# Attention in which the exponentials are transposed by the plain identity and the outputs are divided by the softmax sums once per eight heads

## The chip, the cores and the metric

The kernel runs on one core of a Trainium2 chip. The metric is the device time of one execution in microseconds, as the median of several runs.

## The reference, cut to what matters

Two layers of a diffusion backbone over 512 latent tokens ("lat", four tiles of 128) and 256 context tokens ("ctx", two tiles), model width 1024, everything in float32. Each layer has attention in two head groups, an output projection, and an expert retrieval (PEER). For the change only the two attentions count:

```python
# group A, 8 heads: keys are 256 context + 512 latent tokens
s = jnp.einsum('bqhd,bkhd->bhqk', qblk, k_all).astype(jnp.float32) * MLA_QK ** -0.5
p = jax.nn.softmax(s, axis=-1)
o = jnp.einsum('bhqk,bkhd->bqhd', p, v_all)
# group B, 8 heads: context keys + a window of +-128 tokens + one sink logit per head
p = softmax(concatenate([s_ctx, s_loc, s_sink]))      # s scaled by SWA_DIM ** -0.5, the sink not
o = p[..., :C] @ vc + p[..., C:C + nk] @ vblk
```

So each output row of a head is (exponentials times values) divided by the sum of the exponentials, where in group B the sum also has the exponential of the head's sink. Context tokens attend to context alone.

## The kernel before

The work is cut into token tiles of 128. For each tile there are generators: `KV` and `Q` (normalise, project, rotate), `A` (attention, function `attend`), `O` (output projection, line 561), `R` (routing: 16 products with `wq` at line 630 and top-16 searches on VectorE) and `G`/`GH` (choice of experts; one-hot matrices at lines 826 to 840). The main loop strings them together; `par` interleaves two or three of them by weights. There are ten calls of `attend`: two context tiles and four latent tiles in layer 0, four latent tiles in layer 1.

The experts of some tiles are fetched row by row: `experts` issues one indirect transfer of 512 KB per row on GpSimd's queue (line 740) into one of five buffers, and VectorE multiplies it (line 744, a dot product, or line 754, an addition). The experts of the other tiles go through a dense stage (lines 854 to 914), whose order is written out by hand. Nearly half of the gathered rows are issued ahead of the dense stage and fill the time of the stages before it. Outside the dense stage the order of each engine's instructions is set by a planner that simulates the engines; each engine then runs its list strictly in that order.

`attend` goes over four pairs of heads of group A, then four pairs of group B. For each head: the scores go to a `big` accumulator (two of them; lines 526, 541, 544, 547); `soft` takes the row maximum on VectorE (line 476), turns it into a negative bias by one small VectorE instruction (line 482) or, with a sink, two (lines 479 and 480), runs the exponential on ScalarE with the sum as a by-product (line 485), with a sink adds its exponential (lines 488, 489), takes the reciprocal of the sum (line 490) and makes on ScalarE a 128x128 diagonal matrix `dsu` of it (line 492, three buffers). `pair_pv` then turns each 128x128 block of exponentials (line 504): the product of the block with that diagonal matrix is the block transposed and divided by the sums at once. ScalarE copies two blocks of both heads to `peT` (line 508), line 511 multiplies the values by them, and line 513 copies a pair's 128x128 output into `oT`, which `O` reads in eight slices `k`, accumulated in order. The transposes elsewhere (`heads_T`, line 358, and line 464) use the transpose instruction with `ident`. Line 504 is:

```python
nc.tensor.matmul(pt[:, (2 * b + x) * P:(2 * b + x + 1) * P],
                 pe[x][0][:, (b0 + b) * P:(b0 + b + 1) * P], pe[x][1], start=True, stop=True)
```

`pt` is one of two `m1` accumulators, which the routing and the projections use too.

## Time and profile before

| what | value |
|---|---|
| median of 3 runs | 4539.35 us (4536.53 to 4549.56) |
| the profiled execution's own time | 4543.53 us |
| its span, first to last instruction | 4541.7 us |
| mean granted TensorE clock | 0.899 of 2.4 GHz |
| busy: TensorE, VectorE, ScalarE, GpSimd | 82%, 74%, 38%, 37% |
| instructions | 59277, of them 20350 matmuls |

The stretches of attention lie at about 163 to 289 us, 540 to 1284 us and 2757 to 3476 us of the span; the two dense stages lie at about 1400 to 2530 us and 3600 to 4541 us. A share of busy time is a mean over stages with different limits. "The chain" below is the chain of work that ended last, followed back from the last instruction: at each step to what released it, or to the instruction before it on its engine.

### The profile page before, as it was taken

How to read it: one execution, taken by the hardware profiler on the slowest of the kernel's cores; microseconds unless marked ns; L12 is line 12 of the kernel's file. 1: busy time of each engine (PE TensorE's matmuls, PEld its weight loads, DVE VectorE, ACT ScalarE, POOL GpSimd, SP SyncE). 2: the span in 40 equal slices, each digit the busy share in tenths (PEclk: the TensorE clock that was granted, in tenths of full speed). 3: DMA queues.
4: the chain of work that ended last, by engine and by line, in shares of the span. 5: the costliest groups of instructions: out<-in, count | busy, mean ns of one | idle time of the engine just before them, and what ended most of it. 6: DMA issues, size and time to landing. Idle time of an engine off the chain costs nothing.

```text
span 4541.7 us, 59277 instructions
## 1 busy us (share of the span) xinstructions
PE 3707.9 (82%) x20350; PEld 2990.2 (66%) x20350; DVE 3376.4 (74%) x7838; ACT 1731.3 (38%) x3402; POOL 1659.9 (37%) x1402
## 2 busy tenths in 40 slices
PE   6886689478987999999999578677686798888886
PEld 2454358356777888888988445555475787777775
DVE  1247778989678788877888723777997777787887
ACT  1332232156675333333333234233264743333332
POOL 2115565544002444444444500265542014444443
PEclk9987779688987999999999789787887899999998
DMA  8578899889566998999999842798997579999997
GB/s 313 173 248 305 304 336 325 293 313 318 189 211 224 324 322 312 329 326 328 333 313 317 320 150 85 260 343 323 319 337 240 195 265 329 328 331 322 324 321 261
DMA packets 467487, 1306.56 MB, mean 288 GB/s; under 512 B 41568, under 2 KB 147808, under 8 KB 467184
## 3 DMA queue, kind: packets, MB, share of 16 engines
q0 software_dynamic: 199744, 726.26, 45.5%
q1 hardware_dynamic: 267440, 576.50, 36.3%
q8 instruction: 160, 2.62, 0.2%
q14 instruction: 143, 1.17, 0.1%
HBM read 1240.70 MB, written 61.90 MB: 287 GB/s over the span
## 4 chain that ended last, share of the span: by engine, by line
issue 28%; PE 26%; DVE 18%; DMA 11%; POOL 9%; ACT 6%; SPq 0%; POOLq 0%; DVEq 0%; ACTq 0%
POOL gv L740 9%; DVE vacc L754 5%; PE m L630 4%; DMA gv<-v,idx 3%; DVE gv L744 3%; PE m L504 3%; PE m L368 2%; PE A L908 2%; PE o L881 2%; DMA gv<-u,idx 2%; PE m L511 1%; DVE v L855 1%; ACT u L854 1%; DMA w<-w_in 1%; PE big L526 1%
## 5 line engine op out<-in xcount | busy, mean ns | idle before, releaser
L740 POOL DMA_INDIRECT gv<-u,idx x640 | 800.3, 1250 | 1136.5 <-DVE a L744 610.2
L740 POOL DMA_INDIRECT gv<-v,idx x640 | 797.0, 1245 | 931.5 <-DVE vacc L754 593.9
L881 PE MATMUL o<-v,W 128*128 128x512 f32 x3840 | 967.3, 405 | 163.2 <-ACT W L854 161.0
L908 PE MATMUL A<-b,u 128*128 128x384 f32 (+1 forms) x6144 | 954.9, 311 | 21.7 <-ACT w L911 18.7
L908 PEld LDWEIGHTS A<-b,u 128*128 128x128 f32 x6144 | 931.7, 191 | 47.6 <-ACT w L911 25.2
L881 PEld LDWEIGHTS o<-v,W 128*128 128x128 f32 x3840 | 729.1, 194 | 338.7 <-ACT W L854 185.4
L754 DVE SCALAR_TENSOR_TENSOR vacc<-gv,a,vacc 128x1024 f32<-128x1024 f32 x635 | 812.6, 1280 | 51.7 <-DMA gv<-v,idx 39.8
L744 DVE CUSTOM_DVE_ANT_0 gv<-gv,btok 128x1024 f32<-128x1024 f32 x640 | 764.8, 1220 | 77.8 <-DMA gv<-u,idx 75.0
L854 ACT ACTIVATE W<-w 128x384 fp32r<-128x384 f32 (+1 forms) x256 | 120.7, 471 | 1117.3 <-DVE w L914 1117.3
L855 DVE TENSOR_TENSOR u<-raw,u 128x1024 fp32r<-128x1024 f32 x256 | 313.7, 1226 | 161.6 <-ACT u L854 158.9
L368 PE MATMUL m<-w,aT 128*128 128x256 f32 (+3 forms) x704 | 271.1, 536 | 105.7 <-DMA w<-w_in 55.2
L855 DVE TENSOR_TENSOR v<-raw,v 128x1024 fp32r<-128x1024 f32 x256 | 312.2, 1219 | 7.0 <-ACT v L854 7.0
L630 PE MATMUL m<-bT,wq 128*128 128x128 f32 x2560 | 313.1, 278 | 2.2 <-ACT bT L274 1.4
L630 PEld LDWEIGHTS m<-bT,wq 128*128 128x128 f32 x2560 | 300.7, 194 | 7.3 <-issue 4.2
L368 PEld LDWEIGHTS m<-w,aT 128*128 128x128 f32 x704 | 149.9, 223 | 215.7 <-DMA w<-w_in 78.9
L854 ACT ACTIVATE u<-raw 128x1024 fp32r<-128x1024 f32 x256 | 267.6, 1045 | 46.8 <-DMA raw<-uT 46.6
L854 ACT ACTIVATE v<-raw 128x1024 fp32r<-128x1024 f32 x256 | 267.6, 1045 | 9.8 <-PE o L881 8.3
L855 DVE TENSOR_TENSOR W<-w,W 128x384 fp32r<-128x384 f32 (+1 forms) x256 | 126.0, 492 | 151.0 <-ACT W L854 148.5
L504 PE MATMUL m<-dsu,pexp 128*128 128x128 f32 x1472 | 220.9, 294 | 8.0 <-ACT peT L508 5.4
L504 PEld LDWEIGHTS m<-dsu,pexp 128*128 128x128 f32 x1472 | 191.8, 201 | 38.1 <-issue 23.4
L526 PE MATMUL big<-kT,qT 96*128 96x256 f32 (+1 forms) x288 | 140.7, 629 | 69.7 <-ACT pexp L485 52.3
L914 DVE TENSOR_TENSOR w<-w,G 128x192 f32<-128x192 f32 (+1 forms) x512 | 143.6, 320 | 69.9 <-DMA G<-Gd 45.7
(211 smaller groups left out, 4343.4 us busy)
## 6 DMA issues: line engine op xcount, KB each, us to landing
raw<-uT SPq DMA_DIRECT2D x256, 512.0 KB
raw<-v SPq DMA_DIRECT2D x256, 512.0 KB
wq<-wq SPq DMA_DIRECT2D x144, 512.0 KB
gv<-ada_w POOLq DMA_DIRECT2D x80, 512.0 KB
Gd<-ar SPq DMA_DIRECT2D x80, 512.0 KB
w<-w_out SPq DMA_DIRECT2D x72, 512.0 KB
G<-Gd SPq DMA_DIRECT2D x16, 1536.0 KB
G<-Gd SPq DMA_DIRECT2D x16, 1024.0 KB
```

The lines of the kernel that those rows point to most:

```text
L368: nc.tensor.matmul(ps[:, :cn], aT[:, k, :], w[k][:, :cn], start=(k == 0), stop=(k == KC - 1))
L504: nc.tensor.matmul(pt[:, (2 * b + x) * P:(2 * b + x + 1) * P], pe[x][0][:, (b0 + b) * P:(b0 + b + 1) * P], pe[x][1], start=True, stop=True)
L526: nc.tensor.matmul(ps[:, k0:k0 + n], qT[:, h, :], kv["kT"][:, h, k0:k0 + n], start=True, stop=True)
L630: nc.tensor.matmul(ps[:, c], w[:, k, :], bT[:, k, :], start=(k == 0), stop=(k == KC - 1))
L740: return t, nc.gpsimd.indirect_dma_start(out=t, out_offset=None, in_=src, in_offset=bass.IndirectOffsetOnAxis(ap=idx[:, k:k + 1], axis=0))
L744: ins = nc.vector.tensor_tensor_reduce(out=t, in0=t, in1=bt, scale=1.0, scalar=0.0, op0=OP.mult, op1=OP.add, accum_out=a[:, k:k + 1])
L754: return nc.vector.scalar_tensor_tensor(acc, t, w[:, k:k + 1], acc, op0=OP.mult, op1=OP.add)
L854: nc.scalar.activation(hi, x, AF.Copy)
L855: nc.vector.tensor_tensor(lo, x, hi.bitcast(F32), OP.subtract)
L881: nc.tensor.matmul(acc[t][x], W[:, a_, c], v[:, b_, x * 512:(x + 1) * 512], start=(e == 0 and (a_, b_) == PARTS[0]), stop=(e == NK - 1 and ...
L908: nc.tensor.matmul(A, u[:, a_, k * P:(k + 1) * P], b[:, b_, k], start=(k == 0 and (a_, b_) == PARTS[0]), stop=(k == KC - 1 and (a_, b_) == ...
L914: nc.vector.tensor_tensor(wv[:, x], wv[:, x], gc[x][:, :, e % GC, :], OP.mult)
```

## The change

The blocks of exponentials are turned by the transpose instruction with the plain identity, so they stay undivided. The diagonal matrix and the reciprocal per head are gone. The sums of eight heads are collected in one 128x8 tile, and a new function `over_sums`, called twice in each `attend`, takes one reciprocal of the tile, spreads it over the rows of the outputs by eight small products with the identity (values as 64 equal columns, into one `m1` accumulator), and multiplies four 128x128 slices of `oT` by it in place.

The scales of the scores (1/sqrt(96) and 1/sqrt(64)) move into the gains by which the queries are already multiplied as they are copied. With them gone from `soft`, the negated maximum comes straight out of the reduction; in group B one more instruction takes its minimum with the negated sink.

```diff
--- before.py
+++ after.py
@@ -286,15 +286,20 @@
         g = cst.tile([P, n], F32, tag="gains", name="gains")
         src = I["gains"]
         nc.sync.dma_start(g, bass.AP(tensor=src.tensor, offset=src.offset + l * n, ap=[[0, P], [1, n]]))
-        k["sink"] = g[:, 2 * QK + 2 * SD:]
+        k["nsink"] = g[:, 2 * QK + 2 * SD:]
+        nc.vector.tensor_scalar(k["nsink"], k["nsink"], -1.0, None, op0=OP.mult)
         k["g_mq"], k["g_mk"] = g[:, NOPE:QK], g[:, QK + NOPE:2 * QK]
         k["g_sq"], k["g_sk"] = g[:, 2 * QK:2 * QK + SD], g[:, 2 * QK + SD:2 * QK + 2 * SD]
         cols = cst.tile([P, 9], F32, tag="gcols", name="gcols")
         nc.sync.dma_start(cols, I["gcols"][l])
         k["qa_g"], k["kva_g"] = cols[:, 0:3], cols[:, 3:5]
+
+        nc.vector.tensor_scalar(cols[:, 5:6], cols[:, 5:6], QK ** -0.5, None, op0=OP.mult)
+        nc.vector.tensor_scalar(cols[:, 7:8], cols[:, 7:8], SD ** -0.5, None, op0=OP.mult)
         k["mq_ctx"], k["mk_ctx"], k["sq_ctx"], k["sk_ctx"] = (cols[:, i:i + 1] for i in range(5, 9))
         lat = cst.tile([P, 2], F32, tag="glat", name="glat")
-        nc.vector.memset(lat, 1.0)
+        nc.vector.memset(lat[:, 0:1], QK ** -0.5)
+        nc.vector.memset(lat[:, 1:2], 1.0)
         nc.vector.tensor_copy(lat[:NOPE, :], cols[:NOPE, 5:7])
         k["mq_lat"], k["mk_lat"] = lat[:, 0:1], lat[:, 1:2]
         return k
@@ -464,33 +469,25 @@
                 nc.tensor.transpose(pt[:, c * P:(c + 1) * P],
                                     q[:, 2 * c:2 * c + 2, :].rearrange("p h w -> p (h w)"), ident)
             nc.scalar.activation(sqT[j], pt.rearrange("p (c t) -> p c t", t=P), AF.Copy,
-                                 scale=1.0 if st == "lat" else K["sq_ctx"])
+                                 scale=SD ** -0.5 if st == "lat" else K["sq_ctx"])
             yield
         for j, i in enumerate(tiles):
             qs[st, i] = qT[j], sqT[j]
 
 
-    def soft(ps, n, scale, sink):
-
-        m = sm.tile([P, 1], F32, tag="mx", name="mx")
-        nc.vector.reduce_max(m, ps[:, :n], axis=AX.X)
-        nb = sm.tile([P, 1], F32, tag="nb", name="nb")
-        if sink is not None:
-            nc.vector.tensor_scalar(m, m, scale, sink, op0=OP.mult, op1=OP.max)
-            nc.vector.tensor_scalar(nb, m, -1.0, None, op0=OP.mult)
-        else:
-            nc.vector.tensor_scalar(nb, m, -scale, None, op0=OP.mult)
+    def soft(ps, n, su, nsink):
+
+        nb = sm.tile([P, 1], F32, tag="nb", name="nb", bufs=4)
+        nc.vector.tensor_reduce(nb, ps[:, :n], AX.X, OP.max, negate=True)
+        if nsink is not None:
+            nc.vector.tensor_scalar(nb, nb, nsink, None, op0=OP.min)
         e = tm("pexp", (P, H * QK), bufs=PEXP)
-        su = sm.tile([P, 1], F32, tag="su", name="su")
-        nc.scalar.activation(e[:, :n], ps[:, :n], AF.Exp, bias=nb, scale=scale, accum_out=su)
-        if sink is not None:
+        nc.scalar.activation(e[:, :n], ps[:, :n], AF.Exp, bias=nb, accum_out=su)
+        if nsink is not None:
             es = sm.tile([P, 1], F32, tag="es", name="es")
-            nc.scalar.activation(es, sink, AF.Exp, bias=nb, scale=1.0)
+            nc.scalar.activation(es, nsink, AF.Exp, bias=nb, scale=-1.0)
             nc.vector.tensor_tensor(su, su, es, OP.add)
-        nc.vector.reciprocal(su, su)
-        d = sm.tile([P, P], F32, tag="dsu", name="dsu", bufs=3)
-        nc.scalar.activation(d, ident, AF.Copy, scale=su)
-        return e, d
+        return e
 
     def pair_pv(pe, n, vof, dst):
 
@@ -501,8 +498,8 @@
             pt = m1()
             for b in range(bn):
                 for x in range(2):
-                    nc.tensor.matmul(pt[:, (2 * b + x) * P:(2 * b + x + 1) * P],
-                                     pe[x][0][:, (b0 + b) * P:(b0 + b + 1) * P], pe[x][1], start=True, stop=True)
+                    nc.tensor.transpose(pt[:, (2 * b + x) * P:(2 * b + x + 1) * P],
+                                        pe[x][:, (b0 + b) * P:(b0 + b + 1) * P], ident)
             eT = tm("peT", (P, 4, P), bufs=3)
             dv = eT[:, :2 * bn, :].rearrange("p b t -> p (b t)")
             nc.scalar.activation(dv, pt[:, :2 * bn * P], AF.Copy)
@@ -512,10 +509,24 @@
                                      start=(b0 + b == 0), stop=(b0 + b == nb - 1))
         nc.scalar.activation(dst, po, AF.Copy)
 
+    def over_sums(o, su):
+
+
+        rs = sm.tile([P, H], F32, tag="rsu", name="rsu")
+        nc.vector.reciprocal(rs, su)
+        pr = m1()
+        for c in range(H // 2):
+            for x in range(2):
+                nc.tensor.matmul(pr[x * VD:(x + 1) * VD, c * P:(c + 1) * P],
+                                 rs[:, 2 * c + x:2 * c + x + 1].to_broadcast([P, VD]), ident, start=True, stop=True)
+        ov = o.rearrange("p c t -> p (c t)")
+        nc.vector.tensor_tensor(ov, ov, pr, OP.mult)
+
     def attend(l, st, i, qT, sqT, K, kv):
 
         nk = C if st == "ctx" else C + S
         oT = fm_tile("oT")
+        su = sm.tile([P, H], F32, tag="su", name="su")
         for c in range(H // 2):
             yield
             pe = []
@@ -525,9 +536,11 @@
                     n = min(512, nk - k0)
                     nc.tensor.matmul(ps[:, k0:k0 + n], qT[:, h, :], kv["kT"][:, h, k0:k0 + n],
                                      start=True, stop=True)
-                pe.append(soft(ps, nk, QK ** -0.5, None))
+                pe.append(soft(ps, nk, su[:, h:h + 1], None))
             pair_pv(pe, nk, lambda x, kt: kv["v"][:, kt, (2 * c + x) * VD:(2 * c + x + 1) * VD],
                     oT[:, c, :])
+        over_sums(oT[:, 0:4, :], su)
+        su = sm.tile([P, H], F32, tag="su", name="su")
         j0, j1 = (0, 0) if st == "ctx" else (max(0, i - 1), min(NT[st], i + 2))
         nk2 = C + (j1 - j0) * P
         for c in range(H // 2):
@@ -545,9 +558,11 @@
                                      start=True, stop=(j == i))
                     if j != i:
                         nc.tensor.matmul(dst, identb, mlo if j < i else mhi, start=False, stop=True)
-                pe.append(soft(ps, nk2, SD ** -0.5, K["sink"][:, 2 * c + x:2 * c + x + 1]))
+                h = 2 * c + x
+                pe.append(soft(ps, nk2, su[:, h:h + 1], K["nsink"][:, h:h + 1]))
             pair_pv(pe, nk2, lambda x, kt: kv["sv"][:, kt if kt < 2 else kt + j0, g * SD:(g + 1) * SD],
                     oT[:, 4 + c, :])
+        over_sums(oT[:, 4:8, :], su)
         return oT
 
     def out_proj(l, tiles, oT, m):
```

## Rows read from the trace of the kernel before

**Rows 1.** The page: the engines' busy time, and their shares of the chain.
```profile
PE 3707.9 (82%) x20350; PEld 2990.2 (66%) x20350; DVE 3376.4 (74%) x7838; ACT 1731.3 (38%) x3402; POOL 1659.9 (37%) x1402
...
issue 28%; PE 26%; DVE 18%; DMA 11%; POOL 9%; ACT 6%; SPq 0%; POOLq 0%; DVEq 0%; ACTq 0%
```

**Rows 2.** Busy us by stretch: PE, PEld, DVE, ACT, POOL; PEclk, DMA share, GB/s.
```profile
163.00:212.00 49.00, 44.60 (x239) 22.84 (x240) 15.45 (x70) 27.94 (x85) 8.45 (x16) 0.93 0.58 196
650.00:864.00 214.00, 151.59 (x1074) 127.87 (x1073) 188.18 (x505) 51.27 (x117) 118.02 (x102) 0.81 0.90 319
967.00:1134.00 167.00, 142.93 (x998) 119.43 (x996) 151.86 (x467) 105.94 (x238) 72.32 (x64) 0.87 0.90 324
1400.00:2530.00 1130.00, 1087.09 (x5410) 979.55 (x5410) 916.52 (x1293) 383.06 (x542) 486.72 (x378) 0.98 0.91 316
2757.00:2819.00 62.00, 59.23 (x417) 43.62 (x418) 19.71 (x70) 36.78 (x89) 0.00 (x0) 0.97 0.14 46
2939.00:3009.00 70.00, 68.44 (x475) 49.77 (x476) 60.09 (x140) 35.89 (x90) 48.64 (x37) 0.96 0.83 286
3312.00:3476.00 164.00, 121.37 (x833) 102.33 (x832) 149.98 (x429) 103.72 (x235) 63.76 (x61) 0.82 0.88 312
```

**Rows 3.** The chain by line, whole execution, share of its span.
```profile
by line: issue 28.2%; POOL gv L740 9.1%; DVE vacc L754 5.0%; PE m L630 4.5%; DMA gv<-v,idx 3.2%; DVE gv L744 3.2%; PE m L504 2.7%; PE m L368 2.5%; PE A L908 2.4%; PE o L881 2.1%; DMA gv<-u,idx 1.9%; PE m L511 1.5%; DVE v L855 1.5%; ACT u L8
```

**Rows 4.** The chain by line, stretch 2757 to 2819, and four of its pieces.
```profile
by line: PE m L504 31.3%; PE m L511 17.6%; PE big L526 15.1%; PE big L561 11.5%; PE big L541 8.1%; PE big L544 5.7%; ACT L485 4.1%; ACT pexp L485 3.2%; PE big L547 2.1%; issue 1.2%; PE m L421 0.7%; ACT oT L513 0.5%; ACT peT L508 0.0%; ACTq 
...
2772.04 1.76 PE m L504 x14
...
2780.96 0.59 PE m L511 x8
2781.55 1.09 PE m L504 x8
...
2784.82 1.02 PE m L511 x16
```

**Rows 5.** The chain by line, stretch 163 to 212.
```profile
by line: PE acc L209 25.0%; PE m L504 19.4%; PE big L561 13.1%; PE big L541 10.2%; PE m L511 9.6%; PE big L526 9.0%; ACT L485 2.6%; ACT L242 2.6%; PE m L464 2.3%; ACT pexp L485 2.1%; DVE q L461 1.4%; ACT pexp L324 1.3%; ACT q L458 1.0%; ACT
```

**Rows 6.** The chain by line, stretch 2939 to 3009.
```profile
by line: PE m L504 33.5%; PE m L511 18.7%; PE big L526 15.1%; PE big L561 9.9%; PE big L544 9.8%; PE big L541 7.2%; PE big L547 3.5%; ACT L485 1.8%; ACT pexp L485 1.4%; PE m L464 0.6%; ACT oT L513 0.4%; issue 0.2%
```

**Rows 7.** Groups by line and shape, TensorE: busy, mean ns, idle before.
```profile
L504 PE MATMUL m<-dsu,pexp 128*128 128x128 f32 x1472 | 220.9, 294 | 8.0 <-ACT peT L508 5.4 <-ACT pq L636 1.9 <-ACT dsu L492 0.7
...
L511 PE MATMUL m<-peT,v 128*64 128x128 f32 x832 | 69.9, 300 | 5.2 <-DVE mrep L613 5.1
...
L511 PE MATMUL m<-peT,sv 128*64 128x128 f32 x640 | 57.0, 319 | 72.1 <-DVE mrep L613 72.0
...
L358 PE MATMUL m<-ident,q 128*96 128x128 f32 x176 | 31.4, 338 | 46.2 <-DVE q L447 23.3 <-DVE q L403 20.0 <-DVE q L451 2.8
```

**Rows 8.** TensorE in order of time, 2700 to 2705.
```profile
2701.17 1.04 PE L358 MATMUL m<-ident,q 128*96 128x128 f32 x8
```

**Rows 9.** Groups by line and shape, ScalarE and VectorE.
```profile
L744 DVE CUSTOM_DVE_ANT_0 gv<-gv,btok 128x1024 f32<-128x1024 f32 x640 | 764.8, 1220 | 77.8 <-DMA gv<-u,idx 75.0 <-issue 1.3 <-DVE a L744 0.4
...
L492 ACT ACTIVATE dsu<-ident,su 128x128 f32<-128x128 f32 x160 | 62.9, 398 | 74.1 <-PE m L504 35.7 <-DVE su L490 33.1 <-issue 2.3
...
L490 DVE RECIPROCAL su<-su 128x1 f32<-128x1 f32 x160 | 24.8, 156 | 44.0 <-ACT pexp L485 43.1
...
L570 DVE TENSOR_TENSOR upd<-big,gate 128x512 f32<-128x512 f32 x20 | 13.7, 686 | 40.3 <-PE big L561 23.0 <-DMA gate<-gate 17.2
...
L482 DVE TENSOR_SCALAR nb<-mx 128x1 f32<-128x1 f32 x80 | 11.6, 146 | 0.6
...
L243 DVE RECIPROCAL hss<-hss 128x8 f32<-128x8 f32 x32 | 6.3, 197 | 5.9 <-ACT hss L242 5.9
```

**Rows 10.** TensorE in order of time, 2817 to 2819.
```profile
2818.66 0.70 PE L561 MATMUL big<-w,oT 128*128 128x512 f32 x1 [0.38 <-ACT oT L513]
```

## The prediction

> **What bounds the kernel now.** I read the page's first and fourth parts, then the busy time by stretch, then the chain inside the stretches of attention, then the groups of instructions of lines 476 to 513.
>
> By the page TensorE is busy 82% and VectorE 74%, but the chain that ended last lies on TensorE for 26%, on VectorE for 18% and on ScalarE for 6% [rows 1]. No engine sets the end alone, so the change has to be priced stretch by stretch. The dense stage shows 1087 us of TensorE in 1130 [rows 2]; none of the changed lines run there, so I leave both dense stages as they are.
>
> The attentions show two kinds of stretch. In 163 to 212, 2757 to 2819 and 2939 to 3009 attention runs alone or nearly so, TensorE is busy for 91 to 98% at a granted clock of 0.93 to 0.97 (that is, almost wholly at 2.4 GHz), and VectorE, where it is full, is full of gathered rows that could be done at another time. In 650 to 864, 967 to 1134 and 3312 to 3476 attention, routing and gathers share the core: VectorE is busy 88 to 91% of the time, TensorE 71 to 86% at a clock of 0.81 to 0.87, and the transfers' share is 0.88 to 0.90 [rows 2].
>
> Of the whole chain, line 504 (turning the exponentials) holds 2.7%, or 123 us, and line 511 holds 1.5%, or 68 us [rows 3]. In the three quiet stretches line 504 is 31.3% [rows 4], 19.4% [rows 5] and 33.5% [rows 6] of the chain, and nearly all the rest is TensorE too. So there TensorE's own work sets the pace.
>
> **Removed: one of two instructions per turned block.** Blocks turned, by the code: a latent tile has 6 key blocks for each of 8 heads of group A (48) and 4, 5, 5 or 4 window blocks for each of 8 heads of group B, so a layer has 4 x 48 + 32 + 40 + 40 + 32 = 336, two layers 672; two context tiles with 2 blocks for 16 heads add 64. That is 736, and the trace shows 1472 matmuls of line 504, as well as 832 + 640 = 1472 of line 511: each float32 product is two instructions. The transposes of line 358 are 8 per call in 22 calls, 176, and the trace shows 176 [rows 7]. A transpose is one instruction.
>
> What one costs: eight transposes of line 358 took 1.04 us [rows 8], eight instructions of line 504 took 1.09 us on the chain and fourteen 1.76, so 0.112 us for each further one [rows 4]. One transpose costs about as much as one of the two instructions of a product. So 736 instructions go and the other 736 cost what they did. The line's 123 us on the chain become 61: **-61 us**. Lower bound of the gain: only the three quiet stretches, where line 504 holds 0.194 x 49 + 0.313 x 62 + 0.335 x 70 = 52 us of the chain [rows 4 to 6], half of it, -26. Upper bound: half of the line's whole busy time of 220.9 us, -110 [rows 7].
>
> The Trainium skill, "Perfetto Trace Analysis", section "Transposes", says a logical transpose should be issued as one because it skips the arithmetic, and "TensorE: Matmul & The Clock Gate", section "Terms", gives the transposing mode as four times faster for float32. By that factor three quarters of the line's 123 us would go, 92 instead of 61; the rows of line 358 show a half, so I go by them.
>
> **Added on TensorE.** `over_sums` runs twice in each of ten calls, eight products of two instructions each: 20 x 16 = 320, of line 511's shape (64 columns of weights). Sixteen of those took 1.02 us on the chain [rows 4], so 20.4 us of work. Line 511 has 68 us on the chain for 1472 x 1.02 / 16 = 94 us of work, 72%; by that share **+15 us** (bounds 0 and +20).
>
> **ScalarE.** The 160 diagonal matrices go, 62.9 us busy [rows 9]. ScalarE's busy 1731 us stand for 6% of 4541.7, or 272 us, on the chain [rows 1], one sixth: **-10 us** (bounds 0 and -63). These instructions also stood still for 74.1 us, 35.7 of it waiting for line 504 to free one of the three `dsu` buffers, with the exponentials and copies queued behind them [rows 9]; that is in no term above and is the second rival.
>
> **VectorE.** 160 reciprocals go (24.8 us) and 80 negations without a sink (11.6); with a sink, two small instructions become one, so another 80 of line 482's 146 ns, 11.6 us, go as well (line 480 is that instruction on the other branch). Added: 20 times a reciprocal of 128x8 at 197 ns and a product of 128x512 with an accumulator at 686 ns [rows 9], 17.7 us, and four column operations more per layer, under 2. Net -29. VectorE has 18%, or 817 us, of the chain for 3376 us of busy time [rows 1], a quarter: **-7 us** (bounds 0 and -29). The negated reduction itself isn't in the trace; I take it as dear as the plain one, since it reads the same accumulator; one small instruction's 146 ns [rows 9] more or less on 160 would be 23 us of VectorE, a quarter of it, 6, on the chain. The scales moved into the gains change operands of instructions that are there anyway: 0.
>
> **A new wait.** The last copy into `oT` freed the output projection after 0.38 us [rows 10]. Now VectorE's product stands between them: 0.69 us, and if a gathered row has just started, up to 1.22 more [rows 9]. Behind it in VectorE's list wait the rows and the next maxima; the accumulator that it reads is one of the two `m1` that line 504 alternates. In the middle of `attend` the next group's scores cover it; at the end the slices `k` 0 to 3 of the projection can. Twenty times 0 to 1.9 us; I take 0.4, as most calls have that cover: **+8 us** (0 to +38).
>
> **Sum.** -61 + 15 - 10 - 7 + 8 = -55. In the shared stretches VectorE and the transfers are right behind at 88 to 91% [rows 2], so a shortened chain soon meets another; I give back 5: **-50 us**. From the profiled execution's 4543.5 that is 4493; the runs shown have a median 4.2 lower, so 4489, given as **4490**.
>
> **Rivals.**
>
> Gathers bind the shared stretches. VectorE's 188 of 214 us and the transfers' 0.90 [rows 2] speak for it; against it, that rows can move to later stages, and line 504 is on the chain there too. Then only the quiet stretches gain: -26 and +6 for `over_sums`, -20: 4519.
>
> The stalls count too. With the 74.1 us of ScalarE's standing and 44.0 of the reciprocals' [rows 9] gone, exponentials come earlier; if half of ScalarE's 74 reaches the end, -87: 4452. Against it: in the quiet stretches TensorE had no idle time that this could fill.
>
> The clock falls (the rival on the other side). TensorE with less to do and new waits would look as in 650 to 864, where it had 71% busy and 0.81 granted, so part of it at 1.2 GHz [rows 2]. Work at that level takes twice as long. The three quiet stretches hold some 160 us of TensorE's work after the change; each us of it at the lower level costs one more. From 64 us on it is slower beyond what can be told; at 80 it is +30: 4569. Against it: what remains there is still mostly back to back.
>
> The transposes also come as two instructions. Then +15 - 10 - 7 + 8 = +6: 4545. Against it: the 176 of line 358 [rows 7].
>
> TensorE only looks full. Its weight loads are busy 43.6 of 62 us in 2757 to 2819 against 59.2 for its products [rows 2]; were the smaller share its true load, waits would set the pace and line 504's half would bring nothing: -10 - 7 + 8 = -9, 4530. The chain's pieces, which follow each other on TensorE almost without a gap, speak against it [rows 4]. "Perfetto Trace Analysis" of the Trainium skill, section "Identifying the Most-Contended Engine", asks to judge TensorE by its weight loads and not by matmul busy time; by that rule this rival would hold, and the chain in the rows does not bear it out.
>
> **How the numbers follow.** The forecast 0.57 (its own range 4460 to 4518), gathers 0.16, stalls 0.12, clock 0.08, two instructions 0.03, slack 0.04. A measurement of this kernel can tell about 0.3%, 14 us, from no change. Faster: 0.57 + 0.12 + two thirds of the gathers' case, 0.11 = 0.80; same: 0.05 + 0.03 + 0.04 = 0.12; slower 0.08. The range 4438 to 4524 takes in the forecast, most of the stalls' and of the gathers' case, and leaves out 0.2.
>
> **What the profile after would show.** The turning line has 736 matmuls of 272 to 300 ns and half the share of the chain; 320 new small ones; no `dsu`; ScalarE some 63 us less busy, VectorE some 29 less, TensorE some 80 (half of line 504's 220.9, less 320 times line 511's mean share of 127 us for 1472). The stretches alone, 2757 to 2819 and 2939 to 3009, are 7 to 8 us shorter each (80 or 88 instructions less at 0.112, two `over_sums` at 1.0). It would be wrong if the granted clock fell there, if TensorE waited for line 508's copies or `over_sums` for long, or if the planner, which orders everything outside the dense stages anew from changed times, put gathered rows so that the dense stages start no earlier.

## Result and the profile after

The changed kernel took 4506.08 us (median of 5 runs, 4492.62 to 4511.88) against 4539.35 us before (now of five runs, with the same median and range). The ratio is 0.9913 with a 95% interval of 0.989 to 0.9937: 29 to 50 us less. The forecast of 4490 lies 16 us below the median, the median lies inside the range, and the direction is right.

The profiled execution of after is the fastest of its five (4492.62 us), so the two traces lie 51 us apart, 18 us more than the medians do. Executions of one kernel lie up to 34 us apart (the kernel before took 4522 to 4556 us in 17 of them), and each trace is a single one, so a place in a trace that moves by ten us or so may have moved by chance. Places and lengths are read from the traces below; what an edit is worth at the end is read from the ratios.

The page of after, engines' busy time and their shares of the chain, to be set against [rows 1]:

```profile
PE 3648.8 (81%) x19934; PEld 2933.2 (65%) x19934; DVE 3360.1 (75%) x7566; ACT 1688.3 (38%) x3246; POOL 1669.6 (37%) x1402
...
PE 39%; issue 18%; DVE 17%; DMA 13%; ACT 7%; POOL 6%; SPq 1%; POOLq 0%; DVEq 0%; ACTq 0%
```

416 matmuls are gone (20350 to 19934): 736 less for the turning, 320 new. On the page TensorE is 59 us less busy, ScalarE 43, VectorE 16, where some 80, 63 and 29 were forecast; the rows of the changed lines themselves come nearer (below). Now the groups by line and shape. After's lines have moved: turning is line 501, the copies to `peT` 505, the products with the values 508, the copies to `oT` 510, `over_sums` 516 to 523, the scores 537 to 560, the output projection 576:

```profile
L501 PE MATMUL m<-ident,pexp 128*128 128x128 f32 x736 | 124.5, 294 | 6.1 <-ACT peT L505 3.9 <-ACT pq L651 1.9
...
L520 PE MATMUL m<-ident,rsu 128*64 128x128 f32 x320 | 23.8, 287 | 0.0
```

```profile
L483 DVE TENSOR_SCALAR nb<-nb,gains 128x1 f32<-128x1 f32 x80 | 16.5, 209 | 0.8
...
L523 DVE TENSOR_TENSOR oT<-oT,m 128x512 f32<-128x512 f32 x20 | 13.6, 680 | 13.0 <-ACT oT L510 12.5 <-PE m L520 0.5
```

Against [rows 7], half of the turning instructions are gone, at the same 294 ns each, and 320 small products have come, for 23.8 us: 72.6 us of matmuls less. On VectorE the product of line 523 takes 680 ns, as read off line 570. ScalarE has no `dsu` row any more (62.9 us in [rows 9]). The page's busy times fell by less than these rows because lines that the change doesn't touch took longer (the dense stage's products with `W` 981 us in after, 967 before), because ScalarE has four more table loads (54 instead of 50, 1.3 us each), and because the page counts instructions that overlap on an engine only once: added up one by one, ScalarE's fell by 57 us and VectorE's by 37.

Next the busy time by stretch (columns as in [rows 2]); the first two are quiet, the other two shared:

```profile
2731.00:2781.00 50.00, 46.70 (x362) 33.10 (x362) 16.21 (x38) 30.84 (x72) 0.00 (x0) 0.97 0.13 41
2901.00:2961.00 60.00, 57.08 (x412) 38.75 (x412) 53.16 (x107) 33.78 (x76) 40.27 (x30) 0.92 0.82 273
...
625.00:830.00 205.00, 147.85 (x1028) 124.71 (x1028) 180.79 (x455) 47.24 (x104) 115.48 (x96) 0.79 0.88 317
941.00:1113.00 172.00, 138.28 (x946) 114.69 (x945) 149.23 (x441) 105.57 (x229) 73.05 (x64) 0.83 0.85 304
```

The first is the attention that [rows 2] show at 2757 to 2819. It fits into 50 us where it had 62; TensorE is still busy for 93% of it, at a granted clock of 0.97 as before. The chain inside it, with four of its pieces:

```profile
by line: PE m L508 21.4%; PE m L501 19.2%; PE big L537 10.9%; PE big L554 10.1%; PE big L557 7.1%; PE big L576 6.9%; ACT pexp L485 5.8%; PE m L520 3.8%; PE big L560 2.6%; ACT L242 2.6%; ACT L485 2.6%; issue 2.2%; DVE nb L481 1.8%; DVE oT L5
...
2746.02 1.02 PE m L501 x8
...
2778.44 1.02 PE m L520 x16
2779.46 0.90 PE m L508 x16
2780.69 0.70 DVE oT L523
```

Turning fell from 31.3% of 62 us to 19.2% of 50, from 19.4 us to 9.6: a half. Eight turning instructions take 1.02 us where eight of the old kind took 1.09 [rows 4], so a transpose costs about what one of a product's two instructions cost. The Trainium skill's factor of four ("TensorE: Matmul & The Clock Gate", section "Terms") is not borne out by these rows, which show a factor of two.

Lengths of the ten calls of `attend` in the traces, from the start of the first exponential to the end of the last copy into `oT`, in us (c: context tile, t: latent tile of layer 0, T: of layer 1; the five quiet ones first):

| trace | c0 | c1 | t0 | T0 | T1 | sum of five | t1 | t2 | t3 | T2 | T3 |
|---|---|---|---|---|---|---|---|---|---|---|---|
| before | 47.0 | 85.8 | 78.5 | 60.7 | 69.6 | 341.6 | 212.5 | 167.2 | 157.9 | 145.4 | 219.7 |
| after | 37.7 | 79.0 | 57.4 | 49.7 | 59.9 | 283.7 | 203.9 | 170.9 | 158.0 | 132.3 | 209.2 |
| E1, products kept | 44.8 | 76.7 | 69.5 | 59.6 | 72.8 | 323.4 | 214.4 | 155.8 | 163.8 | 139.4 | 216.1 |
| E3, small fold alone | 43.1 | 80.7 | 76.2 | 60.7 | 72.6 | 333.3 | 216.7 | 165.3 | 158.9 | 141.6 | 215.5 |
| E5, quiet calls alone | 38.1 | 79.8 | 59.1 | 49.7 | 64.5 | 291.2 | 212.5 | 168.8 | 161.6 | 144.8 | 219.0 |

Three of the five quiet calls are the prediction's quiet stretches: c0, T0 and T1. In t0 TensorE is busy for 95% as well, in both traces. c1 is the least quiet: routing of the other context tile runs beside it, and TensorE is busy for 91% before and 88% after. The five together are 58 us shorter, the five shared ones 28, yet this execution is only 51 us shorter and the medians only 33. Where it goes is seen in the starts of the dense stages. The first product line of the dense stage, 908 before and 923 after, in the first and in the second layer:

```profile
L908 PE MATMUL A<-b,u x3072: 333/334/686, 1418.5 to 2520.6; 128*128 128x384 f32 x192
...
L908 PE MATMUL A<-b,u x3072: 274/283/579, 3605.0 to 4507.0; 128*128 128x256 f32 x192
```

```profile
L923 PE MATMUL A<-b,u x3072: 333/334/687, 1400.1 to 2505.1; 128*128 128x384 f32 x192
...
L923 PE MATMUL A<-b,u x3072: 274/283/579, 3556.0 to 4456.2; 128*128 128x256 f32 x192
```

In layer 0 the attention of t0 ends 32 us earlier, but the dense stage starts only 18 us earlier: 14 were lost in the shared stretch between. The dense stage itself gives back 3 more (1105 us from first to last start, against 1102). Layer 1 gains the rest, from 15 us ahead at the end of the first dense stage to 49 at the start of the second: 34, of which T0 and T1 have 21. The second dense stage takes 900 us against 902.

### The profile page after: what moved, and what is told of

It reads as the page before. It is cut to its first block, busy times and chain, and to the rows that moved or that the text cites. A ratio compares the mean times of both kernels' runs of the same rounds, so it can differ in the third digit from the quotient of the medians.

```text
span 4490.8 us, 58079 instructions
## 1 busy us (share of the span) xinstructions
PE 3648.8 (81%) x19934; PEld 2933.2 (65%) x19934; DVE 3360.1 (75%) x7566; ACT 1688.3 (38%) x3246; POOL 1669.6 (37%) x1402
## 4 chain that ended last, share of the span: by engine, by line
PE 39%; issue 18%; DVE 17%; DMA 13%; ACT 7%; POOL 6%; SPq 1%; POOLq 0%; DVEq 0%; ACTq 0%
PE A L923 9%; PE o L896 8%; POOL gv L755 6%; DVE vacc L769 5%; PE m L645 5%; DMA gv<-v,idx 3%; DVE gv L759 3%; PE m L373 3%; DMA raw<-uT 2%; DMA gv<-u,idx 2%; PE acc L854 2%; DMA w<-w_in 2%; DVE v L870 2%; ACT ar L855 1%; PE m L501 1%
## 5 line engine op out<-in xcount | busy, mean ns | idle before, releaser
L896 PE MATMUL o<-v,W 128*128 128x512 f32 x3840 | 981.2, 409 | 147.6 <-ACT W L869 147.3
L896 PEld LDWEIGHTS o<-v,W 128*128 128x128 f32 x3840 | 739.8, 196 | 322.2 <-ACT W L869 169.8
L373 PE MATMUL m<-w,aT 128*128 128x256 f32 (+3 forms) x704 | 259.3, 517 | 81.1 <-DMA w<-w_in 48.4
L481 DVE TENSOR_REDUCE nb<-big 128x1 f32<-128x768 f32 (+3 forms) x160 | 122.0, 765 | 89.2 <-PE big L537 42.4
L505 ACT ACTIVATE peT<-m 128x512 f32<-128x512 f32 (+1 forms) x192 | 109.7, 576 | 202.1 <-PE m L508 105.5
```

Source lines behind the costliest of these rows:

```text
L373: nc.tensor.matmul(ps[:, :cn], aT[:, k, :], w[k][:, :cn], start=(k == 0), stop=(k == KC - 1))
L481: nc.vector.tensor_reduce(nb, ps[:, :n], AX.X, OP.max, negate=True)
L896: nc.tensor.matmul(acc[t][x], W[:, a_, c], v[:, b_, x * 512:(x + 1) * 512], start=(e == 0 and (a_, b_) == PARTS[0]), stop=(e == NK - 1 and ...
```

## The experiments

Each row has the median, the ratio to the kernel before on the same chip with its 95% interval, and what that is in us of 4540.

| label | edit | median us | ratio | change, us |
|---|---|---|---|---|
| (after) | the whole change | 4506.08 | 0.9913 [0.989, 0.9937] | -39 |
| E1 | after, turned by products | 4547.49 | 1.0019 [1.0005, 1.0034] | +9 |
| E2 | after, no `over_sums` | 4495.77 | 0.9899 [0.988, 0.9919] | -46 |
| E3 | before with the small fold alone | 4513.36 | 0.9945 [0.9925, 0.9966] | -25 |
| E4 | after, projection in another order | 4500.70 | 0.9907 [0.9886, 0.9927] | -42 |
| E5 | new way in the quiet calls | 4511.15 | 0.9928 [0.9912, 0.9945] | -33 |
| E6 | new way in the shared calls | 4537.97 | 0.9994 [0.9984, 1.0005] | -3 |
| E7 | after, with diagonal matrices that nobody reads | 4514.46 | 0.9933 [0.9915, 0.9951] | -30 |
| N1 | before, ten small instructions more | 4543.31 | 1.0006 [0.9994, 1.0019] | +3 |
| E8 | after, fewer rows ahead | 4517.50 | 0.9943 [0.9929, 0.9957] | -26 |
| N2 | before, fewer rows ahead | 4554.27 | 1.0022 [1.0006, 1.0038] | +10 |
| E9 | E3 with the saved VectorE work put back | 4519.09 | 0.9946 [0.9931, 0.9961] | -25 |
| E10 | after, other weights of `attend` in the order | 4498.49 | 0.9896 [0.988, 0.9913] | -47 |

The difference between two of these has an uncertainty of 8 to 14 us (the two half widths of 0.001 to 0.0024 combined), so a difference of less says only that the effect is no larger than some 20.

**E1: is it the halving, or all that goes with the diagonal matrices?**

```diff
-                    nc.tensor.transpose(pt[...], pe[x][...], ident)
+                    nc.tensor.matmul(pt[...], pe[x][...], ident, start=True, stop=True)
```

> The changed kernel with one edit undone: the blocks of exponentials are multiplied by the plain identity instead of transposed, so each is two TensorE instructions again; over_sums, the folded scales and the missing diagonal matrices stay. Theory 1 (the halved turning pays, 61 us on the chain by the working of the prediction): 736 instructions come back, and the time goes up to that of the kernel before or a little over it, 4535 to 4555 us. Theory 2 (the shorter way from the scores to the turned block pays: no reciprocal, no diagonal matrix, one small VectorE step less, and TensorE has slack): the time stays at the changed kernel's 4506, within 10 us.

Measured: 1.0019, 9 us above before. The group of its turning line, and a piece of its chain at 2754 to 2814, the same attention as above:

```profile
L501 PE MATMUL m<-ident,pexp 128*128 128x128 f32 x1472 | 217.0, 292 | 5.4 <-ACT peT L505 4.1 <-ACT pq L651 0.9
```

```profile
by line: PE m L501 34.6%; PE m L508 18.4%; PE big L537 17.8%; PE big L554 8.3%; PE big L557 6.2%; PE big L576 5.8%; PE m L520 3.2%; PE big L560 2.2%; ACT L485 2.1%; ACT pexp L485 1.7%; DVE oT L523 1.2%; PE m L426 0.7%; ACT oT L510 0.5%; iss
...
2766.09 1.09 PE m L501 x8
```

Without the halving nothing is gained in this build: all the rest of the change together, with the diagonal matrices, the reciprocals and their stalls gone, brings no time. The rival that the stalls count too forecast -87 for the whole; without the halving's 61 it would still gain 26 here, where 9 were lost. The attention of T0 takes 59.6 us against 49.7 in after: 9.9 for 80 instructions, 0.124 each.

**E2: what does the division cost?** It leaves the division by the sums out.

```diff
-        over_sums(oT[:, 0:4, :], su)
...
-        over_sums(oT[:, 4:8, :], su)
```

> The changed kernel without over_sums: the outputs of the heads are not divided by their sums at all, and the reciprocal, the 320 small products and the 20 products on VectorE are left out. If over_sums costs what the prediction put down (15 us of TensorE on the chain, and 8 of the new wait, less a little of VectorE): 23 to 28 us below the changed kernel, so about 4480. If it lies wholly beside other work: within 5 us of 4506. If the wait before the output projection is worth the 19 to 21 us that the profile after shows TensorE idle there, and the small products too: 35 us or more, 4470 or below.

Measured: 6 us less than after by the ratios, 10 by the medians, where the sum had +15 for the products and +8 for the wait. With an uncertainty of 14 on the 6, the two cost between nothing and some 20, less than the 23 together. T0 takes 50.6 us without the division and 49.7 with it, so there it cost nothing that could be seen.

**E3: the small fold alone.** The kernel before, with the scales in the gains and the maximum negated in the reduction; diagonal matrices, reciprocals and products stay.

```diff
-        nc.vector.reduce_max(m, ps[:, :n], axis=AX.X)
...
+        nc.vector.tensor_reduce(nb, ps[:, :n], AX.X, OP.max, negate=True)
+        if nsink is not None:
+            nc.vector.tensor_scalar(nb, nb, nsink, None, op0=OP.min)
...
         nc.vector.reciprocal(su, su)
         d = sm.tile([P, P], F32, tag="dsu", name="dsu", bufs=3)
         nc.scalar.activation(d, ident, AF.Copy, scale=su)
```

> Only the small part of the change: scales folded into the gains, the negated maximum straight from the reduction, one step with the sink; but the reciprocal per head, the diagonal matrix and the product by it stay, and there is no over_sums. 160 small VectorE instructions of about 146 ns go, and nothing else. Theory 1: 23 us of VectorE, a quarter of it on the chain, so 4 to 8 us below the kernel before, 4531 to 4535. Theory 2 (the hops between maximum and exponential pay): half or more of the gain, 4523 or below.

Measured: -25, three times and more what was expected. In its trace the five quiet calls are only 8 us shorter; its dense stages start at the times of the two rows below, 18 and 33 us earlier than before, so most of the gain arises outside those calls. Its diagonal matrices are all there, with their stalls:

```profile
L495 ACT ACTIVATE dsu<-ident,su 128x128 f32<-128x128 f32 x160 | 63.3, 399 | 65.9 <-PE m L509 39.9 <-DVE su L493 22.6 <-DVE nb L482 3.0
```

```profile
L939 PE MATMUL A<-b,u x3072: 333/334/687, 1400.1 to 2496.2; 128*128 128x384 f32 x192
...
L939 PE MATMUL A<-b,u x3072: 274/283/582, 3571.9 to 4473.0; 128*128 128x256 f32 x192
```

**E9: is the fold's gain VectorE's work?** E3, and for each head one 128x1 product on VectorE whose result nobody reads.

```diff
         nc.vector.tensor_reduce(nb, ps[:, :n], AX.X, OP.max, negate=True)
+        mx = sm.tile([P, 1], F32, tag="mx", name="mx")
+        nc.vector.tensor_scalar(mx, eps_t, -1.0, None, op0=OP.mult)
```

> The kernel with only the folded scales (25 us below the kernel before, against 4 to 8 expected) and one added instruction per head: a 128x1 product on VectorE of the kind that the folding removed, read by nobody and on nobody's way. VectorE's list is as long as before; the way from the maximum to the exponential stays short. If VectorE's busy time was the gain: 4533 to 4545. If the shorter way was: 4510 to 4520. If it was the luck of the planner's order, there is no reason to come out at either; 4525 to 4545 then, most likely, as the halves of the change do when added up.

Measured: 0.9946, the same as E3. So the gain is not VectorE's busy time. Two causes are left: the shorter way from the maximum to the exponential, and the planner's order. On TensorE the orders of E3 and E9 agree from 56 to some 1300 us of the span, so E9 doesn't tell these two apart. The traces say something against the first. From the end of a maximum to the start of its exponential the median of 160 heads is 3.2 us before, 2.6 in E3 and 2.7 in E9, but 2.4 in E1 and 2.3 in E6, and neither of these two is more than a few us faster than before. So the shorter way does not bring 25 us by itself.

**E4: does the wait before the output projection cost?** After, with slices `k` 0 to 3 of both halves first, then 4 to 7.

```diff
-        for n in range(2):
-            w = big_w(I["w_out"][l][:, n * 512:(n + 1) * 512], 512)
...
+        for k0 in (0, 4):
+            for n in range(2):
+                w = big_w(I["w_out"][l][k0 * P:(k0 + 4) * P, n * 512:(n + 1) * 512], 512)
```

> The changed kernel with another order in the output projection: slices k 0 to 3 for both halves of the columns first, then k 4 to 7 for both, so that twice as much work that does not need the second over_sums lies ahead of the wait for it (same matmuls, same bytes, weights in half-height pieces). Seven waits of TensorE there add up to 19.1 us in the profile after. If that wait counts: 8 to 18 us below the changed kernel, 4488 to 4498. If other work covers it, or the projection then waits for its weights instead: within 5 us of 4506.

Measured: 0.9907 against 0.9913. The wait is in after's trace; those who waited for the product of line 523:

```profile
PEld big L576: 21.5, 8
PE big L576: 19.1, 7
```

So TensorE stands 19 us before line 576 in 7 places, 2.7 each, more than the 0.4 by twenty of the sum. E4's own trace has the same rows, and the wait is still there for the most part:

```profile
PEld big L577: 16.3, 7
PE big L577: 13.7, 7
```

The edit took 5 of the 19 us away, and the time changed by 3, which can't be told from nothing. So E4 says little of what the wait costs; the bound comes from E2, where the wait and the products are both gone and at most some 20 us are won.

**E5 and E6: quiet calls alone, shared calls alone.** The new way in some calls of `attend`, the diagonal matrix and the product in the others; the small fold in all.

```diff
+DG = [(0, 'lat', 1), (0, 'lat', 2), (0, 'lat', 3), (1, 'lat', 2), (1, 'lat', 3)]                       # E5
+DG = [(0, 'ctx', 0), (0, 'ctx', 1), (0, 'lat', 0), (1, 'lat', 0), (1, 'lat', 1)]                       # E6
...
+        dg = (l, st, i) in DG
...
+                    if dg:
+                        nc.tensor.matmul(o_, i_, pe[x][1], start=True, stop=True)
+                    else:
+                        nc.tensor.transpose(o_, i_, ident)
```

> The changed kernel, with the division by diagonal matrices and the product of the kernel before kept in five of the ten calls of attend: those that share the core with routing and gathers (latent tiles 1, 2 and 3 of layer 0, tiles 2 and 3 of layer 1). The new way stays in the five quiet calls. Theory 1 with the gathers binding the shared stretches (a rival of the prediction): nearly all of the changed kernel's gain stays, 4505 to 4520. Theory 1 alone, by the share of the chain and of the blocks (312 of 736 in the quiet calls): 15 to 20 us below the kernel before, and up to 25 with the folded scales, 4516 to 4526. If the planner's new order counts as much as the change itself: anywhere between 4500 and 4545, and the stretches that no edit touches move by 10 us and more.

> The counterpart: the new way only in the five calls that share the core, the old division in the five quiet ones. Gathers binding: 4525 to 4540. By the share of blocks (424 of 736): 4510 to 4525. The two halves' gains should add up to about the changed kernel's 33 us, counting the folded scales once, if order effects are small; if they do not add up within some 10 us, the order counts.

Measured: -33 for the quiet calls, -3 (+2 to -7) for the shared ones. The quiet calls turn 312 blocks (64 in the two context tiles, 80 each in t0 and T0, 88 in T1), the other five calls the remaining 424. Against E1, which has all but the halving, the 312 bring 41 us (1.0019 less 0.9928) and the 424 bring 11 (1.0019 less 0.9994), where their instructions on TensorE, at 0.112, are 35 and 47 us of work. (E1 has `over_sums` in all ten calls, E5 and E6 keep the matrices in five, so they differ in that too.) E3 is the other base: the same source as E5 and E6 with all ten calls in the list `DG`. Against it the quiet calls bring 8 us (0.9945 less 0.9928, within the uncertainty of 12), the shared ones cost 22 (0.9994 less 0.9945, clear of its 10), and both together, in after, bring 15 (uncertainty 14). So by both bases the gain comes from the quiet calls and the shared ones bring little or nothing, but what the quiet ones bring at the end is 41 by one and 8 by the other. The parts don't add up by E3: with the fold counted once the two halves make -11, where the whole makes -39, and by what was written down before the run that means that the order counts.

**E7: ScalarE's diagonal matrices.** After, with 160 of them again, read by nobody.

```diff
+        d = sm.tile([P, P], F32, tag="dsu", name="dsu", bufs=3)
+        nc.scalar.activation(d, ident, AF.Copy, scale=nb)
```

> The changed kernel with the 160 diagonal matrices on ScalarE put back, made from the bias and read by nobody, so that ScalarE has its 63 us of work again but no instruction waits for TensorE to free a buffer. The computation is the same otherwise. If ScalarE's work is what the prediction put down: about 10 us above the changed kernel, 4512 to 4520. If ScalarE has room everywhere: 4506, within 5. If ScalarE's time was the better part of the gain (theory 2): 4530 or more.

Measured: 9 us above after by the ratios, 8 by the medians. That agrees with the term of 10, though with its uncertainty of 13 it can't be told from nothing. The matrices' own row shows that they take the time of before:

```profile
L491 ACT ACTIVATE dsu<-ident,nb 128x128 f32<-128x128 f32 x160 | 63.0, 394 | 78.0 <-DVE nb L481 77.9
```

**N1: does any edit move the time by reordering?** Before, with a 128x1 memset in each `attend`.

```diff
         oT = fm_tile("oT")
+        mk = sm.tile([P, 1], F32, tag="mk", name="mk")
+        nc.vector.memset(mk, 0.0)
```

> The kernel before with ten added instructions, a 128x1 constant written by VectorE at the start of each attend and read by nobody: about 1 us of work, but the planner orders everything outside the dense stages anew. If the order that the planner happens to find is worth little: within 5 us of the kernel before, 4534 to 4546. If it is worth as much as the effects looked for here: 10 us or more away, on either side, with the difference in stretches where nothing was changed.

Measured: 1.0006, no change. The order on TensorE hardly moved (behind a few swaps in the first 56 us it is the same), so this is a weak test: it shows that two builds with nearly one order agree.

**E8 and N2: do gathered rows pace the stages before the dense ones?** After and before, with fewer of the rows issued ahead.

```diff
-AHEAD = (0.46, 0.5)
+AHEAD = (0.44, 0.47)
```

> The changed kernel with 16 gathered rows fewer ahead of each dense stage (0.44 and 0.47 of them instead of 0.46 and 0.50); those rows run within the dense stages instead. If the gathers set the pace of the stretches that attention shares with routing (some 2 us per row there by the count of gathers per 100 us): up to 32 us less ahead of each dense stage, and the dense stages, where VectorE has a fifth of its time free, give back less than half of it: 10 to 30 us below 4506. If something else sets the pace there: within 6 us of 4506, or above it by what the dense stages lose.

> The kernel before with the same 16 rows fewer ahead of each dense stage. If the gathers pace the shared stretches in the kernel before as well: as much below 4541 as the changed kernel gains from it. If only the changed kernel, with its shorter quiet stretches, has too many rows ahead: within 6 us of 4541 or above it.

Measured: E8 is 14 us slower than after, N2 10 us slower than before. E8's dense stages:

```profile
L923 PE MATMUL A<-b,u x3072: 331/334/687, 1381.3 to 2501.2; 128*128 128x384 f32 x192
...
L923 PE MATMUL A<-b,u x3072: 274/283/582, 3551.3 to 4476.6; 128*128 128x256 f32 x192
```

In layer 0 the dense stage starts 19 us earlier than after's, and then takes 15 us longer (1120 against 1105); in layer 1 it starts 5 earlier and takes 25 longer. N2 does the same to the kernel before: its dense stages start at 1408.2 and 3583.2, 10 and 22 us earlier, and take 18 and 27 longer. Up to some 1130 us E8 has after's order on TensorE (but for swaps before 56), and by then it is 17 ahead. All in all the stages before the dense ones win 20 us in E8's trace and 40 in N2's, and the dense stages lose 40 and 45. So the rows do help to pace what comes before the dense stage, and a row that isn't fetched there is paid for in it.

**E10: the order alone.** After, with the weight of `attend` raised in the five stretches where it shares the core; every instruction stays.

```diff
-                par((A(t, 1), 8), (R((c, 1), (t, 0)), 24))
+                par((A(t, 1), 12), (R((c, 1), (t, 0)), 24))
...
-                par((A(t, 3), 8), (R((t, 2)), 24), (GH(1), 48))
+                par((A(t, 3), 12), (R((t, 2)), 24), (GH(1), 48))
```

> The changed kernel in another order: in the five stretches where attention shares the core, the attention's steps are handed to the planner earlier against the routing's (weight 12 instead of 8). Every instruction is the same. If the order in the shared stretches is worth what the kernels so far suggest, 20 us between like kernels: 8 us or more away from 4506 on either side, all of it between 630 and 1400 us and behind 3070 us. If the order is worth little: within 6 us.

Measured: 4498.49, 0.9896, the lowest median of a kernel that computes everything; against after's 0.9913 it can't be told apart. Its dense stages:

```profile
L923 PE MATMUL A<-b,u x3072: 333/334/689, 1393.1 to 2493.7; 128*128 128x384 f32 x192
...
L923 PE MATMUL A<-b,u x3072: 274/283/582, 3560.9 to 4462.0; 128*128 128x256 f32 x192
```

The last routing products before the first dense stage (lines 630 and 645), in before, after and E10:

```profile
L630 PE MATMUL m<-bT,wq x256: 275/275/370, 1310.8 to 1350.6; 128*128 128x128 f32 x128
```

```profile
L645 PE MATMUL m<-bT,wq x256: 275/275/371, 1294.7 to 1334.9; 128*128 128x128 f32 x128
```

```profile
L645 PE MATMUL m<-bT,wq x256: 274/275/421, 1261.6 to 1300.2; 128*128 128x128 f32 x128
```

In after they end 16 us earlier than before, in E10 50. So the same instructions in another order move the end of this stage by 34 us. Yet E10's dense stage starts only 7 us before after's: 27 of the 34 are lost to what comes between. Its five shared calls take 787 us together against 874 in after, 88 less, and the end hardly moves: the length of a shared call is no measure of what it costs.

## Why the prediction was right

**TensorE binds the quiet stretches: right.** E1 and after differ in one line, and so in 736 instructions; with the products back nothing is left of the gain. The forecast for the attentions at 2757 and 2939 was 7 to 8 us shorter each; they are 11 and 10 shorter. That this is no luck of the order is seen in all fourteen traces. Seven builds turn the blocks of the quiet calls by one instruction (after, E2, E4, E5, E7, E8, E10), seven by two (before, E1, E3, E6, E9, N1, N2). T0 takes 49.6 to 53.1 us in the first seven and 59.6 to 61.8 in the others; the five quiet calls together take 284 to 307 and 323 to 342.

**Removed, -61: right mechanism, too much of it at the end.** The sum took half of line 504's share of the whole chain, 123 us. The part for the quiet calls came: their 312 blocks at the forecast 0.112 us are 35 us, and from E1 to after these calls shorten by 40. Of the 26 left for the shared calls, 3 to 11 came (E6, against before or against E1); against E3 22 were lost. What failed is the step "I give back 5": at least 15 to 23 were given back. The chain's share is a share of one path. Where others run close behind, as VectorE and the transfers do at 88 to 91% [rows 2], halving a piece of that path can move the path more than the end. That is argued and not shown, and the rows have a second cause beside it, the clock. The shared calls t1 and t2, in E1 and in E6:

```profile
647.00:862.00 215.00, 154.56 (x1116) 133.75 (x1115) 190.06 (x461) 47.17 (x104) 119.58 (x103) 0.81 0.90 322
978.00:1134.00 156.00, 131.36 (x997) 111.48 (x998) 139.38 (x419) 93.22 (x206) 69.24 (x61) 0.91 0.89 319
```

```profile
638.00:861.00 223.00, 150.81 (x1028) 126.87 (x1027) 192.66 (x459) 47.33 (x104) 130.50 (x107) 0.77 0.90 320
985.00:1141.00 156.00, 123.75 (x887) 101.74 (x885) 131.98 (x398) 88.14 (x194) 59.48 (x54) 0.86 0.82 291
```

In these calls the two builds differ in the turning alone. With products the granted clock is 0.81 and 0.91 there (0.81 and 0.87 in before [rows 2]), with transposes 0.77 and 0.86 (E6) or 0.79 and 0.83 (after). TensorE, with less to do (busy 72 and 84% of the two in E1, 68 and 79% in E6), was for longer at the lower of its two levels, 1.2 GHz. By an estimate from these rows, busy time by the difference in clock, that takes back 7 to 14 us of the 20 that the 176 blocks of t1 and t2 have at 0.112. No run holds the clock fixed, so which of the two causes it was stays open.

**Luck in the sum.** That 4490 came within 16 us is in part two errors that cancel: 10 to 18 us too little given back, and 13 to 17 us too much for division and wait (below). And if the planner's order gave E3 its 25 us, it may have a share in the 39 as well.

**What does not add up.** With the rest of the change in place the halving is worth 48 us (1.0019 less 0.9913). E1, E5, E6, E7 and E2 fit that: fold, matrices and division together bring nothing, halving brings 41 in the quiet calls and about 11 in the others. E3 and E9 don't fit: by them the fold alone is worth 25 and what is left of the whole change 15, so that E1 should be at -28 with ScalarE's 9 won and the division's 6 lost, and it is at +9, 37 us off; and E6, which has the fold too, should not be at -3. The quiet calls are not where the 37 us are, since they sum to 323 us in E1 and to 333 in E3. Much of it is there before t0 begins. The exponentials of t0, in E1 and E3:

```profile
L485 ACT ACTIVATE pexp<-big,nb x16: 680/788/903, 544.4 to 597.9; 128x768 f32<-128x768 f32 x8, 128x512 f32<-128x512 f32 x8
```

```profile
L486 ACT ACTIVATE pexp<-big,nb x16: 668/786/901, 521.4 to 575.9; 128x768 f32<-128x768 f32 x8, 128x512 f32<-128x512 f32 x8
```

E3 starts them 23 us earlier, and before that only two quiet calls, c0 and c1, have any attention, which are no shorter together in E3 (123.8 us) than in E1 (121.5). TensorE's lists in the two builds differ from some 176 us of the span on, those of E3 and E9 agree to some 1300 us, and E10 shows that order alone moves a stretch by such amounts. So the order fits; that it is the cause was not shown, since the new instructions in the old order were not tried. What the halving is worth at the end therefore stays open between some 15 and 48 us.

**Division +15 and wait +8: both too high.** E2 has 6 to 10 for the two. The wait came longer than forecast where it came, 2.7 us in 7 places; what it cost at the end is within E2's bound and was not shown apart.

**ScalarE -10: agrees with E7's 9,** which is not told from nothing. **VectorE -7: not as a matter of busy time.** E9 shows that putting such work back costs nothing; yet the fold alone brought 25 (E3). The negated reduction is as dear as the plain one, as the sum assumed (949 ns against 952 for 768 columns). The prediction had no term for the way from maximum to exponential, one instruction shorter in every head, and none for the order. The way alone doesn't bring the 25, since E1 and E6 have it as short; that the order does was not shown.

**The rivals.** Gathers bind the shared stretches: that little is gained there held (E6), and the rows help to pace them (E8, N2), but its price of 20 counted only three of the quiet stretches; with all five calls it is E5's 33, between it and the forecast. The stalls: E1 has none of them and gains nothing, E3 has nearly all of them (65.9 us of 74.1) and gains 25, so nothing says that the gain comes from there. The clock: the granted clock was 0.97 and 0.92 in the two quiet stretches shown, against 0.97 and 0.96 [rows 2]; 0.04 of 57 us of TensorE's work is 2 us, so in the quiet stretches, for which the rival was put forward, it is no more than a few us. In the shared ones it fell too, as said above. Two instructions for a transpose: refuted by the 736, and E1 shows what it would have been, +9 for a forecast of +6.

TensorE only looks full: refuted. The weight loads were busy for 70% of the stretch at 2757 and the stretch still shortened by 11 us as 80 of its instructions went. The prediction said that this rival would hold by the Trainium skill ("Perfetto Trace Analysis", section "Identifying the Most-Contended Engine"). That reads too much into it: the section takes the weight loads, beside the share of peak arithmetic, as the measure of how near TensorE is to its peak, and calls the engine with the highest share the most contended one. At 70% that is TensorE here as well, before ScalarE's 59% and VectorE's 32% (36.78 and 19.71 of 62 us), so the rows agree with the section.

## What to carry to other kernels

A float32 product that turns a block takes two instructions, where the transpose takes one of about the same length; a scaling fused into that product must save more than this elsewhere, and dividing once per eight heads was cheaper here. Price an edit by the stretches in which its engine is alone in setting the pace: 312 of the 736 turned blocks lay there and gave most of the gain, while the other 424, next to VectorE and transfers at some 90%, gave a quarter of their work on TensorE at best, and by E3 less than nothing. Look at the granted clock when work is taken from TensorE beside others: part of it can come back as a lower clock. Where a planner orders anew with each edit, parts of a change don't add up: check a part by undoing it in the changed kernel as well as by doing it alone, and compare the length of one quiet stretch over all builds, as for T0, before trusting a difference at the end.

## What the runs showed that was not expected

Folding the scales and the negation, an edit without any saving on TensorE, brought 25 us (E3, 0.9945), and the same with the saved VectorE work put back (E9, 0.9946). Lowering the share of rows fetched ahead of the dense stages from 0.46 to 0.44 and from 0.5 to 0.47 made both kernels slower by 10 to 14 us (E8, N2), although the first dense stage starts 19 us earlier in E8 than in after.
